# Relu and row mean over 67 MB: six tiles taken by blocks of rows in two passes, relu on ScalarE and row sums on VectorE

## The chip, the cores and the metric

The kernel runs on 1 core of one Trainium2 chip. The metric is the device time of an execution in microseconds (us). Before the change it is 164.05 us, the median of 3 runs (163.62 to 164.06). The profile is one execution recorded by the hardware; its span is about 2 us shorter than the time. All times compared below are of fast runs at a granted clock of 1.0 (the share of the full TensorE clock that the profile shows).

## The reference

```python
x = np.random.randn(32, 512, 1024).astype(np.float32)     # 67.11 MB
relu_x = np.maximum(x, 0)
out = np.mean(relu_x, axis=-1).astype(np.float32)         # 32 x 512
```

That is 16384 rows of 1024 numbers. Each of the 128 partitions takes 128 rows, in 8 tiles of 16 rows: a tile is 128 x 16 x 1024 x 4 bytes = 8.4 MB.

## The kernel before

A row is one instruction: relu and sum together, with an accumulator output. Even rows go to ScalarE, odd ones to VectorE. Tiles 0 to 6 are loaded whole, into three buffers in turn; the last tile (7) comes in pieces of 8, 4, 2 and 1 rows and three pieces of the last row, so that little work is left when the last bytes land.

```python
def act_row(nc, src, acc):
    nc.scalar.activation(out=src, in_=src, func=ACT.Relu, accum_out=acc)

def dve_row(nc, src, acc, init=None):
    nc.vector.tensor_scalar(
        out=src, in0=src, scalar1=0.0, scalar2=init,
        op0=ALU.max, op1=ALU.add, accum_out=acc,
    )
...
    in_pool = pools.enter_context(tc.tile_pool(name="in", bufs=3))
    res_pool = pools.enter_context(tc.tile_pool(name="res", bufs=1))
    sums = res_pool.tile([P, J], F32)
    res = res_pool.tile([P, J], F32)
    part = res_pool.tile([P, 10], F32)

    def rows(xt, lo, n, j0):
        for k in range(lo, lo + n):
            j = j0 + k
            (dve_row if j % 2 else act_row)(nc, xt[:, k, :], sums[:, j:j + 1])
...
    for t in range(full):                      # full = 7
        j0 = t * NB                            # NB = 16
        xt = in_pool.tile([P, NB, D], F32, name="xt")
        nc.sync.dma_start(out=xt, in_=xr[:, j0:j0 + NB, :])
        rows(xt, 0, NB, j0)
...
    # the last piece; part[:, 7:8] is ScalarE's share, already times inv
    dve_row(nc, last[:, 768:], part[:, 8:9], init=part[:, 6:7])
    nc.vector.scalar_tensor_tensor(
        out=res[:, J - 1:J], in0=part[:, 8:9], scalar=inv, in1=part[:, 7:8], op0=ALU.mult, op1=ALU.add,
    )
    nc.sync.dma_start(out=outr, in_=res)
```

Of the kernel before, what the change touches and what calls it, by code (L numbers as in the profile page):

```python
# [1 line left out]

# [4 lines left out]

F32 = mybir.dt.float32
ALU = mybir.AluOpType
ACT = mybir.ActivationFunctionType  # L10
# [15 lines that stand above are left out]
def issue_ahead_of_entry_barrier(nc):  # L26


    entry, body = nc.cur_f.blocks[0].instructions, None
    for block in nc.cur_f.blocks[1:]:  # L30
        for k, ins in enumerate(block.instructions):
            if ins.opcode == "DMACopy":
                body, load = block.instructions, k
                break
        if body is not None:
            break
    first = body[load]
    assert first.engine == mybir.EngineType.SP and not first.sync_info.on_wait
    assert all(i.opcode == "DMACopy" or i.engine != first.engine for i in body[:load])
    del body[load]  # L40
    at = next(k for k, i in enumerate(entry) if i.engine == first.engine and i.opcode == "Drain")
    entry.insert(at, first)


@with_exitstack
def kernel(
    ctx: ExitStack,
    tc: tile.TileContext,
    x: bass.AP,
    out: bass.AP,  # L50
):
    nc = tc.nc
    P = nc.NUM_PARTITIONS
    xf = x.flatten_outer_dims()
    R, D = xf.shape
    assert R % P == 0
    J = R // P
    inv = 1.0 / D
    xr = xf.rearrange("(p j) d -> p j d", p=P, j=J)
    outr = out.flatten().rearrange("(p j) -> p j", p=P, j=J)  # L60
    xlast = xr[:, J - 1, :]

    NB = 16
    full = J // NB - 1

    row_pieces = [8, 4, 2, 1]
    assert sum(row_pieces) == NB - 1
    col_pieces = [512, 256, 256]
    assert sum(col_pieces) == D

    pools = ctx.enter_context(ExitStack())
# [12 lines that stand above are left out]
    def finish(lo, hi):  # L84
        nc.gpsimd.tensor_scalar(  # L85
            out=res[:, lo:hi], in0=sums[:, lo:hi], scalar1=inv, scalar2=0.0, op0=ALU.mult, op1=ALU.add,
        )

    for t in range(full):
        j0 = t * NB  # L90
        xt = in_pool.tile([P, NB, D], F32, name="xt")
        nc.sync.dma_start(out=xt, in_=xr[:, j0:j0 + NB, :])  # L92
        rows(xt, 0, NB, j0)

    j0 = full * NB
    xt = in_pool.tile([P, NB, D], F32, name="xt")
    prev, last = xt[:, NB - 2, :], xt[:, NB - 1, :]
    lo = 0
    for n in row_pieces:
        nc.sync.dma_start(out=xt[:, lo:lo + n, :], in_=xr[:, j0 + lo:j0 + lo + n, :])  # L100
        lo += n
    c = 0
    for w in col_pieces:
        nc.sync.dma_start(out=last[:, c:c + w], in_=xlast[:, c:c + w])
        c += w

    finish(0, j0)
    lo = 0
    for n in row_pieces[:-1]:
        rows(xt, lo, n, j0)  # L110
        lo += n
    finish(j0, j0 + lo)



    act_row(nc, prev[:, :512], part[:, 0:1])
    dve_row(nc, prev[:, 512:], part[:, 1:2])
    nc.gpsimd.tensor_scalar(  # L118
        out=res[:, J - 2:J - 1], in0=part[:, 0:1], scalar1=part[:, 1:2], scalar2=inv, op0=ALU.add, op1=ALU.mult,
    )  # L120
    act_row(nc, last[:, :256], part[:, 2:3])
    dve_row(nc, last[:, 256:512], part[:, 3:4])
    nc.gpsimd.tensor_scalar(  # L123
        out=part[:, 4:5], in0=part[:, 2:3], scalar1=inv, scalar2=0.0, op0=ALU.mult, op1=ALU.add,
    )
    act_row(nc, last[:, 512:640], part[:, 5:6])
    dve_row(nc, last[:, 640:768], part[:, 6:7], init=part[:, 3:4])
    nc.scalar.activation(  # L128
        out=part[:, 7:8], in_=part[:, 5:6], func=ACT.Identity, scale=inv, bias=part[:, 4:5],
# [7 lines that stand above are left out]
    pools.close()  # L137
    tc.close()
    tc.compile()
    issue_ahead_of_entry_barrier(nc)  # L140


# [1 line left out]
_INS = ['x']  # L144
_OUTS = [((32, 512), 'float32')]


# [23 lines left out]
```

## Time and profile before

| what | before |
|---|---|
| time, median | 164.05 us |
| span of the profile | 162.1 us |
| VectorE busy | 74.7 us (46%) |
| ScalarE busy | 69.6 us (43%) |
| HBM read over the span | 414 GB/s |
| a tile's arrival | 19.3 to 19.8 us |
| both engines' work on a tile, side by side | 9.2 us |

"Busy" is an average over the whole span and says only who is not the bound. What decides is the last two rows: a tile needs twice as long to arrive as to be used up. The prediction below shows the lines for this. Two more lines belong to the instructions that the change replaces. They are groups by shape; after the bar stand the busy us and the mean ns of one, then the idle time in front.

```profile
L20 DVE TENSOR_SCALAR_CACHE_REDUCE xt<-xt 128x1024 f32<-128x1024 f32 x63 | 72.6, 1215 | 84.6 <-DMA xt<-in_x_dram 84.3
L15 ACT ACTIVATE xt<-xt 128x1024 f32<-128x1024 f32 x63 | 65.6, 1042 | 88.6 <-DMA xt<-in_x_dram 88.6
```

A row costs 1.2 us on VectorE and 1.0 us on ScalarE, and nearly all the idle time of both ends on the arrival of a load.

### The profile page before, as it was taken

To read this page: it belongs to the slowest core of one execution; us is meant where nothing else is said; L and a number is where in the kernel's file an instruction comes from. 1 tells how busy PE (TensorE), PEld (TensorE's weight loads), DVE (VectorE), ACT (ScalarE), POOL (GpSimd) and SP (SyncE) were. 2 spreads that over 40 slices of the span, in tenths; PEclk is the share of its full clock that TensorE was granted. 3 is DMA by queue.
4 is the path that set the end of the run, shared out by engine and by line. 5 is a ranking of instruction groups with operands and counts; after the bars stand their busy time and mean duration, and the time that the engine had idled before them with its cause. 6 is when DMAs were issued, how large, how long until landed. Compare 5 with 4: busy or idle time off the path is not lost.

```text
span 162.1 us, 358 instructions
## 1 busy us (share of the span) xinstructions
DVE 74.7 (46%) x135; ACT 69.6 (43%) x134; POOL 1.2 (1%) x8
## 2 busy tenths in 40 slices
DVE  0000049700795009930199102990049800698993
ACT  3000049500793009910199002980049600696882
POOL 0000000000000000000000000000000000000001
DMA  8996996997997998998998999899898897998980
GB/s 275 501 485 291 518 501 291 501 501 323 469 518 340 437 518 356 420 518 356 420 520 374 404 501 404 388 501 404 388 518 388 388 518 332 437 445 384 420 311 17
DMA packets 2162, 67.19 MB, mean 415 GB/s; under 512 B 240, under 2 KB 624, under 8 KB 880
## 3 DMA queue, kind: packets, MB, share of 16 engines
q1 hardware_dynamic: 2160, 67.18, 96.6%
q14 instruction: 2, 0.02, 0.0%
HBM read 67.11 MB, written 0.07 MB: 414 GB/s over the span
## 4 chain that ended last, share of the span: by engine, by line
DMA 84%; DVE 13%; SPq 1%; issue 0%; DVEq 0%
DMA xt<-in_x_dram 84%; DVE xt L20 13%; SPq L100 1%; DVE res L132 0%; DVEq L20 0%; DVEq L132 0%; SPq L92 0%
## 5 line engine op out<-in xcount | busy, mean ns | idle before, releaser
L20 DVE TENSOR_SCALAR_CACHE_REDUCE xt<-xt 128x1024 f32<-128x1024 f32 (+1 forms) x65 | 73.7, 1195 | 84.7 <-DMA xt<-in_x_dram 84.3
L15 ACT ACTIVATE xt<-xt 128x1024 f32<-128x1024 f32 (+1 forms) x66 | 67.0, 1015 | 88.7 <-DMA xt<-in_x_dram 88.6
L15 ACT ACTIVATION_READ_ACCUMULATOR xt<-xt 128x1 f32 x66 | 12.3, 186 | 0.0
L20 DVE DVE_READ_ACCUMULATOR xt<-xt 128x1 f32 x65 | 5.4, 83 | 0.0
L85 POOL TENSOR_SCALAR res<-sums 128x112 f32<-128x112 f32 (+1 forms) x2 | 0.5, 252 | 156.7 <-DVE xt L20 156.7
L15 ACT ACT_TABLE_LOAD x1 | 1.3, 1283 | 0.8 <-PEq L155 0.8
L20 DVE TENSOR_SCALAR_CACHE_REDUCE xt<-xt,part 128x128 f32<-128x128 f32 (+1 forms) x2 | 0.8, 412 | 0.1
L128 ACT ACTIVATE part<-part 128x1 f32<-128x1 f32 x1 | 0.3, 294 | 0.1
L118 POOL TENSOR_SCALAR res<-part 128x1 f32<-128x1 f32 x1 | 0.3, 264 | 0.5 <-ACT xt L15 0.5
L132 DVE SCALAR_TENSOR_TENSOR res<-part 128x1 f32<-128x1 f32 x1 | 0.2, 159 | 0.1
L123 POOL TENSOR_SCALAR part<-part 128x1 f32<-128x1 f32 x1 | 0.2, 191 | 0.1
L20 DVE DVE_READ_ACCUMULATOR xt<-xt,part 128x1 f32 x2 | 0.2, 83 | 0.0
L155 POOL MEMSET const-bfloat16-1.0<- 128x1 bf16 x1 | 0.1, 101 | 0.0
L155 POOL MEMSET const-uint8-127<- 128x1 uint8 x1 | 0.1, 101 | 0.0
L155 POOL MEMSET const-float32-0.0<- 128x1 f32 x1 | 0.1, 98 | 0.2 <-issue 0.2
L155 POOL MEMSET const-float32-1.0<- 128x1 f32 x1 | 0.1, 98 | 0.0
## 6 DMA issues: line engine op xcount, KB each, us to landing
xt<-in_x_dram SPq DMA_DIRECT2D x1, 4096.0 KB, 39.0
xt<-in_x_dram SPq DMA_DIRECT2D x1, 2048.0 KB, 43.5
xt<-in_x_dram SPq DMA_DIRECT2D x1, 1024.0 KB, 45.5
xt<-in_x_dram SPq DMA_DIRECT2D x1, 512.0 KB, 46.4
xt<-in_x_dram SPq DMA_DIRECT2D x1, 256.0 KB, 46.5
xt<-in_x_dram SPq DMA_DIRECT2D x2, 128.0 KB, 42.7
xt<-in_x_dram SPq DMA_DIRECT2D x7, 49.1
out_dram<-res SPq DMA_DIRECT2D x1, 64.0 KB, 1.5
```

Of the source, the lines that this page charges most:

```text
L15: nc.scalar.activation(out=src, in_=src, func=ACT.Relu, accum_out=acc)
L20: nc.vector.tensor_scalar(out=src, in0=src, scalar1=0.0, scalar2=init, op0=ALU.max, op1=ALU.add, accum_out=acc,)
L85: nc.gpsimd.tensor_scalar(out=res[:, lo:hi], in0=sums[:, lo:hi], scalar1=inv, scalar2=0.0, op0=ALU.mult, op1=ALU.add,)
L100: nc.sync.dma_start(out=xt[:, lo:lo + n, :], in_=xr[:, j0 + lo:j0 + lo + n, :])
L118: nc.gpsimd.tensor_scalar(out=res[:, J - 2:J - 1], in0=part[:, 0:1], scalar1=part[:, 1:2], scalar2=inv, op0=ALU.add, op1=ALU.mult,)
L123: nc.gpsimd.tensor_scalar(out=part[:, 4:5], in0=part[:, 2:3], scalar1=inv, scalar2=0.0, op0=ALU.mult, op1=ALU.add,)
L128: nc.scalar.activation(out=part[:, 7:8], in_=part[:, 5:6], func=ACT.Identity, scale=inv, bias=part[:, 4:5],)
L132: nc.vector.scalar_tensor_tensor(out=res[:, J - 1:J], in0=part[:, 8:9], scalar=inv, in1=part[:, 7:8], op0=ALU.mult, op1=ALU.add,)
L155: nc = _bacc.Bacc("TRN2", target_bir_lowering=False, num_devices=1)
```

## The change

The intent is to replace many small instructions by few large ones: ScalarE does relu on a block of 8 rows, then VectorE makes 8 row sums of the block in one instruction. Tile 5 is split otherwise (two blocks of 6 rows, four rows on ScalarE alone), and tile 6 and the last tile stay row by row.

```diff
+    def block(xt, lo, n, j0):
+        rs = xt[:, lo:lo + n, :]
+        nc.scalar.activation(out=rs, in_=rs, func=ACT.Relu)
+        nc.vector.tensor_reduce(
+            out=sums[:, j0 + lo:j0 + lo + n], in_=rs, axis=mybir.AxisListType.X, op=ALU.add,
+        )
...
-        rows(xt, 0, NB, j0)
+        if t < full - 2:
+            block(xt, 0, 8, j0)
+            block(xt, 8, 8, j0)
+        elif t == full - 2:
+            block(xt, 0, 6, j0)
+            block(xt, 6, 6, j0)
+            for k in range(12, NB):
+                act_row(nc, xt[:, k, :], sums[:, j0 + k:j0 + k + 1])
+        else:
+            rows(xt, 0, NB, j0)
```

## The prediction

> **What bounds the kernel now.** The work is 67.11 MB read once, with a relu and a row sum behind it. I read the page's span table first: neither compute engine is busy half the time, while the DMA row stands at 8 and 9 throughout. The bytes line gives the mean rate. (GB/s dips every third slice: with one load of 64 KB per partition, packets end in step every few microseconds, and 4 us slices beat against that. I read no stall into it.)
>
> ```profile
> span 162.1 us, 358 instructions
> DVE 74.7 (46%) x135; ACT 69.6 (43%) x134; POOL 1.2 (1%) x8
> DMA  8996996997997998998998999899898897998980
> HBM read 67.11 MB, written 0.07 MB: 414 GB/s over the span
> ```
>
> Next the busy table by stretch, cut at the moments when each 8.4 MB tile lands, which I took from the timeline (22.4, 41.7, 61.0, 80.5, 100.3, 119.7 and 139.0 us). Columns: the stretch and its length, busy us of DVE, ACT and POOL with counts, the clock, the DMA share, GB/s.
>
> ```profile
> 22.36:41.68 19.32, 9.20 (x17) 8.42 (x17) 0.00 (x0) 1.00 1.00 434
> 41.68:61.03 19.35, 9.20 (x16) 8.42 (x16) 0.00 (x0) 1.00 1.00 434
> 80.47:100.30 19.83, 9.21 (x16) 8.42 (x16) 0.00 (x0) 1.00 0.98 424
> 100.30:119.70 19.40, 9.20 (x16) 8.45 (x17) 0.00 (x0) 1.00 1.00 432
> ```
>
> A tile takes 19.3 to 19.8 us to arrive at 424 to 434 GB/s with the DMA engines 98 to 100% busy; 9.2 us of VectorE and 8.4 us of ScalarE side by side use it up. Each compute engine then waits about 10 us for the next tile. The bound is the transfer, and it has no holes to fill.
>
> The chain of waits must be read with care. It runs through 9.2 us of VectorE rows twice:
>
> ```profile
> 41.68 9.22 DVE xt L20 x16
> 50.90 0.02 SPq L92
> 50.95 49.27 DMA xt<-in_x_dram
> 100.36 9.22 DVE xt L20 x16
> 110.96 46.35 DMA xt<-in_x_dram
> ```
>
> It says that the load issued at 50.95 waited for VectorE to free its buffer. But it took 49.27 us to land where 19.35 are enough: two loads were in front of it in the queue. That release could come about 30 us later without a gap in the transfer. So the 13% of VectorE in the chain is no time to be won.
>
> Last, the end. From the timeline, VectorE at each arrival; the bracket holds the idle time ahead of a row and what ended it:
>
> ```profile
> 139.06 1.22 DVE L20 TENSOR_SCALAR_CACHE_REDUCE xt<-xt 128x1024 f32<-128x1024 f32 x1 [10.14 <-DMA xt<-in_x_dram]
> 148.78 1.22 DVE L20 TENSOR_SCALAR_CACHE_REDUCE xt<-xt 128x1024 f32<-128x1024 f32 x1 [0.52 <-DMA xt<-in_x_dram]
> 153.35 0.08 DVE L20 DVE_READ_ACCUMULATOR xt<-xt 128x1 f32 x1
> 153.56 1.22 DVE L20 TENSOR_SCALAR_CACHE_REDUCE xt<-xt 128x1024 f32<-128x1024 f32 x1
> ```
>
> From 139 us on VectorE is nearly full: 0.52 us of slack before the piece of 8 rows, 153.56 - 153.43 = 0.13 before that of 4. A delay carried past 139 us and larger than this would reach the end.
>
> **What the Trainium skill says.** (1) "VectorE: DVE Perf Modes", section "The perf-mode tier table (the rule you actually need)": a tensor_reduce runs at 1x for every data type, that is one element per cycle. The trace has no such instruction, but the row sum it replaces goes at the same pace: 685 ns for 512 elements and 1215 for 1024 is (1215 - 685)/512 = 1.035 ns an element, one cycle of the 0.96 GHz that the page gives. (2) "ScalarE: Activation LUTs", section "What ACT_TABLE_LOAD costs": an ACTIVATE with immediate operands takes 186 ns + 0.833 ns an element. The trace agrees: 186 + 1024 x 0.833 = 1039 against 1042 ns. (3) "SBUF — State Buffer", section "Who interferes with whom": DMA and compute engines use separate ports and do not contend. The stretches above fit: 434 GB/s though both engines worked for half of them. (4) "DMA: Bandwidth & Descriptors", section "Where 436 GB/s comes from": the fabric ceiling is 435 GB/s. The measured 434 sits on it, so nothing on the compute side can raise it.
>
> **The change, part by part.** Tiles 0 to 4 go from 16 row instructions to two blocks of 8 rows: ScalarE does relu on a block, then VectorE reads it once for 8 sums. Tile 5 has two blocks of 6 rows and four rows on ScalarE alone. Tile 6 and the last, piecewise tile stay. Nothing about the loads changes but when a buffer comes free.
>
> Removed: 6 tiles x 16 rows x 2 instructions (the row and its accumulator read) = 192. Added: 10 + 10 block instructions, 2 + 2 smaller ones, and 4 rows x 2 = 32. The count falls from 358 to about 198.
>
> ScalarE block: 8192 elements x 0.833 + 186 ns = 7.01 us; a 6-row one 6144 x 0.833 + 186 = 5.30. VectorE block: slope 1.04 ns and a fixed part of 1215 - 1024 x 1.04 = 150 ns give 8192 x 1.04 + 150 = 8.67 us, and 6144 x 1.04 + 150 = 6.54. These are estimates from the durations above.
>
> Work: ScalarE 69.6 - 6 x 8.42 + 10 x 7.01 + 2 x 5.30 + 4 x 1.04 = 104 us (64%). VectorE 74.7 - 6 x 9.20 + 10 x 8.67 + 2 x 6.54 = 119 us (74%). Both do more work, since relu and sum are now two passes, and stay under the span. Per tile it is 14.0 and 17.3 us against 19.4 for the arrival, so neither builds a backlog.
>
> Release of a buffer, with T the landing: first relu to T + 7.0, first sum to T + 15.7, second sum to T + 24.4 (the second relu, done at T + 14.0, is never waited for). Before, T + 9.3. So tile 3's load is issued at 22.4 + 24.4 = 46.8 instead of 31.6, and so on, 15 us later each. The load in front of it (tile 2) lands at 61.0, which leaves 14 us of queued work when the new load arrives. The last tile's pieces take tile 4's buffer, free at 100.3 + 24.4 = 124.7 instead of 109.6, while tile 6 is still streaming until 139.0. All of the added 15 us lies beside queued transfers: cost on the path zero.
>
> The handover to the end: tile 5 lands at 119.7. ScalarE: blocks to 125.0 and 130.3, four rows to 134.5. VectorE: tile 4 to 124.7, then from 125.0 to 131.6 and to 138.1. Tile 6 lands at 139.0: VectorE is free 0.9 us ahead, ScalarE 4.5 us. The tail then runs as before. The sum is zero; I expect 164.0, the median before being 164.05.
>
> **Rivals.** (a) VectorE becomes the bound. It needs a block sum above 19.4/2 = 9.7 us, 12% over my 8.67. Were the reduction at two cycles an element (17.2 us a block), tiles 0 to 4 alone would end at 29.4 + 10 x 17.2 = 201 us and the whole near 245. Against it: the page's 1x and the same slope in the row sums. For it: this case has no trace of the instruction. (b) The late release starves the queue. It would need a release beyond T + 38.7, two arrivals after the landing. Against it: 14 us of margin. If some depth of the queue itself feeds the rate, the stretches would drop from 434 to, say, 420 GB/s, and the time would be some 168. (c) A late handover. VectorE has 0.9 us in hand at 139.0 and 0.52 us more at 148.8; a block sum 8% slower (9.35 us) makes tile 4 end at 126.1 and tile 5 at 140.2, that is 1.2 us late, of which 0.7 us pass 148.8 and the end moves by about half a microsecond, 0.3%. (d) A gain: 160 instructions fewer, no accumulator reads, VectorE writing nothing back into the tile. All this is time of engines that waited 10 us a tile; the first load, the rate and the tail do not see it. To be over 2% faster the transfer would have to be 3.3 us shorter, and at 434 GB/s the 67.11 MB alone take 154.6 us, while the last landing already lies at about 157.3.
>
> **Range and chances.** The runs before spread from 163.62 to 164.06. Rival (c) and the scatter of single tiles (19.32 to 19.83 us) can add or take half a microsecond, so 163.2 to 164.9 should hold 8 times in 10. Slower by over 2% is rival (a) or (b): 4%. Faster by over 2%: 1%.
>
> **What would show it.** Right: about 198 instructions; block relus near 7.0 us and block sums near 8.7; ScalarE near 104 us and VectorE near 119 us busy; loads issued near 47, 66, 85, 105 and 125 us; stretches between landings still 19.3 to 19.8 us at 424 to 434 GB/s; the chain now through a relu and two sums and yet no longer; DMA in front of tile 6's first row. Wrong: a VectorE row at 139 us or later whose wait ended on VectorE's own tile 5 instead of the DMA, a block sum above 9.7 us, or a DMA share under 0.95 in the stretches from 61 us on, where a queue that ran dry would show.

## The result, and the profile after

The changed kernel takes 164.39 us (median of 4 runs, 164.22 to 164.44), the kernel before in the same rounds 164.01 us. The ratio is 1.0027, with a 95% interval of 1.0009 to 1.0044. Ratios here and below are the mean time of one kernel's fast runs over that of the other's of the same rounds, so not quite the ratio of the medians. By the 2% measure nothing changed, but some 0.4 us lie clear of the scatter, and the prediction had no term for them.

The head of the page of the changed kernel, with the DMA row of the 40 slices:

```profile
span 162.4 us, 201 instructions
DVE 119.0 (73%) x51; ACT 103.5 (64%) x58; POOL 1.2 (1%) x8
DMA  7997997997997999899899899799799798999970
HBM read 67.11 MB, written 0.07 MB: 414 GB/s over the span
```

Instructions fell by 157, VectorE's work rose by 44 us and ScalarE's by 34, and the bytes over the span are the same. Work of 78 us was added to the kernel without a visible price. The new instructions by shape, columns as before:

```profile
L93 DVE TENSOR_REDUCE sums<-xt 128x8 f32<-128x8192 f32 x10 | 86.4, 8681 | 37.9 <-ACT xt L92 37.9
L92 ACT ACTIVATE xt<-xt 128x8192 f32<-128x8192 f32 x10 | 69.7, 7021 | 42.1 <-DMA xt<-in_x_dram 42.1
L93 DVE TENSOR_REDUCE sums<-xt 128x6 f32<-128x6144 f32 x2 | 13.0, 6548 | 0.4 <-ACT xt L92 0.4
L92 ACT ACTIVATE xt<-xt 128x6144 f32<-128x6144 f32 x2 | 10.5, 5315 | 5.4 <-DMA xt<-in_x_dram 5.4
```

A block costs 7.02 us on ScalarE and 8.68 on VectorE. ScalarE waits for loads, VectorE for ScalarE: the two now stand one behind the other. The busy table by stretch, cut near the landings (columns as in the prediction):

```profile
61.10:80.50 19.40, 17.33 (x3) 13.95 (x2) 0.00 (x0) 1.00 1.00 432
80.50:99.84 19.34, 17.20 (x3) 13.95 (x2) 0.00 (x0) 1.00 1.00 434
99.84:119.20 19.36, 17.29 (x3) 13.95 (x2) 0.00 (x0) 1.00 1.00 433
```

VectorE works 17.2 to 17.3 us in each 19.4 us, ScalarE 14.0, and the rate is what it was. The chain of waits (start, duration, what) looks quite different all the same:

```profile
41.80 7.04 ACT xt L92
48.86 17.29 DVE sums L93 x2
66.17 33.66 DMA xt<-in_x_dram
99.91 7.04 ACT xt L92
106.97 17.29 DVE sums L93 x2
125.65 31.31 DMA xt<-in_x_dram
```

The page gives this chain as 65% DMA, 23% VectorE and 9% ScalarE; before it was 84% DMA and 13% VectorE. Taken at its word, 24.3 us twice have moved onto the critical path. They have not: the load issued at 66.17 lands 33.66 us later, although it needs 19.35, because another load stood in front of it. The longer release and the shorter stay in the queue cancel: 24.3 + 33.7 = 58.0 us now, 9.2 + 49.3 = 58.5 us before.

The timeline at the handover to the rows (start, duration, instruction, idle time in front and what ended it):

```profile
138.66 1.22 DVE L20 TENSOR_SCALAR_CACHE_REDUCE xt<-xt 128x1024 f32<-128x1024 f32 x1 [1.03 <-DMA xt<-in_x_dram]
148.36 1.22 DVE L20 TENSOR_SCALAR_CACHE_REDUCE xt<-xt 128x1024 f32<-128x1024 f32 x1 [0.49 <-DMA xt<-in_x_dram]
```

VectorE had been free for 1.03 us when tile 6 landed, and the wait ended on the DMA. In this execution tile 6 landed even 0.4 us earlier than in the profile before (138.6 against 139.0). The end shows where that went. First the kernel before:

```profile
159.23 0.08 DVE L20 DVE_READ_ACCUMULATOR xt<-xt,part 128x1 f32 x1
159.43 0.16 DVE L132 SCALAR_TENSOR_TENSOR res<-part 128x1 f32<-128x1 f32 x1
```

Then the changed kernel, the same two instructions:

```profile
158.90 0.08 DVE L20 DVE_READ_ACCUMULATOR xt<-xt,part 128x1 f32 x1
159.52 0.16 DVE L151 SCALAR_TENSOR_TENSOR res<-part 128x1 f32<-128x1 f32 x1 [0.53 <-DVE xt L20]
```

From the end of the accumulator read to the last instruction there were 0.12 us (159.43 - 159.31); now there are 0.53. ScalarE's partial sum, which the last instruction also takes, was done at 158.83, and the chain books 0.47 us of this gap as "issue": waiting for nothing that the profile shows. These 0.41 us are about the size of the whole difference, but one profile doesn't settle the account: tile 6 was 0.4 us ahead here, and the store of the results behind this instruction took 1.8 us from issue to landing instead of 1.5. It took 1.8 to 1.9 us in all four profiles that have the gap, and 1.5 in the other ten; why is not shown. The change doesn't touch the last instruction.

### The profile page after: what moved, and what is told of

Read it like the earlier page. It is cut to its first block, busy times and chain, and to the rows that moved or that the text cites. A ratio compares the mean times of both kernels' runs of the same rounds, so it can differ in the third digit from the quotient of the medians.

```text
span 162.4 us, 201 instructions
## 1 busy us (share of the span) xinstructions
DVE 119.0 (73%) x51; ACT 103.5 (64%) x58; POOL 1.2 (1%) x8
## 4 chain that ended last, share of the span: by engine, by line
DMA 65%; DVE 23%; ACT 9%; SPq 1%; issue 1%; DVEq 0%; ACTq 0%
DMA xt<-in_x_dram 65%; DVE sums L93 21%; ACT xt L92 9%; DVE xt L20 1%; SPq L119 1%; DVE res L151 0%; DVEq L151 0%; ACTq L92 0%
## 5 line engine op out<-in xcount | busy, mean ns | idle before, releaser
L93 DVE TENSOR_REDUCE sums<-xt 128x8 f32<-128x8192 f32 (+1 forms) x12 | 99.4, 8326 | 38.2 <-ACT xt L92 38.2
L92 ACT ACTIVATE xt<-xt 128x8192 f32<-128x8192 f32 (+1 forms) x12 | 80.3, 6737 | 47.5 <-DMA xt<-in_x_dram 47.5
L15 ACT ACTIVATE xt<-xt 128x1024 f32<-128x1024 f32 (+3 forms) x22 | 21.2, 962 | 7.0 <-DMA xt<-in_x_dram 6.9
L20 DVE TENSOR_SCALAR_CACHE_REDUCE xt<-xt 128x1024 f32<-128x1024 f32 (+2 forms) x17 | 18.5, 1138 | 1.9 <-DMA xt<-in_x_dram 1.7
L15 ACT ACTIVATION_READ_ACCUMULATOR xt<-xt 128x1 f32 x22 | 4.1, 187 | 0.0
L20 DVE DVE_READ_ACCUMULATOR xt<-xt 128x1 f32 x17 | 1.4, 83 | 0.0
## 6 DMA issues: line engine op xcount, KB each, us to landing
xt<-in_x_dram SPq DMA_DIRECT2D x7, 33.7
```

The source lines that it names most:

```text
L20: nc.vector.tensor_scalar(out=src, in0=src, scalar1=0.0, scalar2=init, op0=ALU.max, op1=ALU.add, accum_out=acc,)
L92: nc.scalar.activation(out=rs, in_=rs, func=ACT.Relu)
L93: nc.vector.tensor_reduce(out=sums[:, j0 + lo:j0 + lo + n], in_=rs, axis=mybir.AxisListType.X, op=ALU.add,)
```

## The experiments

Three questions: is the longer release really hidden, and by what; what is the row-by-row end worth; where do the 0.4 us come from. Each kernel gave a correct result.

### With two buffers, the changed kernel and the kernel before

If the third buffer hides the release, taking it away must cost only the changed kernel. The edit is the same in both:

```diff
-    in_pool = pools.enter_context(tc.tile_pool(name="in", bufs=3))
+    in_pool = pools.enter_context(tc.tile_pool(name="in", bufs=2))
```

> The changed kernel with two tile buffers instead of three. Theory (the third buffer is what hides the later release): a buffer is free at landing + 24.4 us, but the load in front lands at + 19.4, so the DMA runs dry for about 5 us and pays its start-up, two loads in about 45 us instead of 38.7; carried through to the last tile I get the end some 19 us later, about 183 us (178 to 188). Rival (release time doesn't matter at all, or VectorE is too fast to matter): about 164.

> The kernel before with two tile buffers instead of three. Theory: its release at landing + 9.3 us is ahead of the next landing at + 19.4, so the queue still never runs dry: 164.0, same within 0.5%. Rival (depth of the queue itself feeds the rate): slower by over 1%, with stretches between landings longer than 19.8 us.

The changed kernel took 188.12 us (ratio 1.1475, 1.1456 to 1.1494), the kernel before 163.95 (0.9999, 0.9984 to 1.0014). The rows of the changed kernel with two buffers, from the slices of its page (about 4.7 us each) and from its timeline:

```profile
DMA  9999999950998999995089999999507999999990
41.68 13.95 ACT L92 ACTIVATE xt<-xt 128x8192 f32<-128x8192 f32 x2 [5.37 <-DMA xt<-in_x_dram]
69.08 13.95 ACT L92 ACTIVATE xt<-xt 128x8192 f32<-128x8192 f32 x2 [13.45 <-DMA xt<-in_x_dram]
88.46 13.95 ACT L92 ACTIVATE xt<-xt 128x8192 f32<-128x8192 f32 x2 [5.43 <-DMA xt<-in_x_dram]
```

Now the DMA row has three holes, and the landings alternate between 27.4 us (41.68 to 69.08) and 19.4 us (69.08 to 88.46). So release time is worth nothing while a load stands in the queue, and everything when none does. My estimate of 183 us, up to 188, was too low, if only by 0.1 us at its upper end: I had a load into the empty queue at some 21 us; this kernel's chain shows 22.20 and 22.33. The kernel before with two buffers kept 431 to 435 GB/s in its stretches, so depth of queue beyond one waiting load bought nothing.

### Tiles 0 and 1 as one block of 16 rows

```diff
-            block(xt, 0, 8, j0)
-            block(xt, 8, 8, j0)
+            if t < 2:
+                block(xt, 0, NB, j0)
+            else:
+                block(xt, 0, 8, j0)
+                block(xt, 8, 8, j0)
```

> The changed kernel with tiles 0 and 1 as one block of 16 rows: relu about 13.8 us, then a sum of about 17.2 us, so their buffers come free at landing + 31 us instead of + 24.4. Theory (the release is hidden while it comes before the load in front has landed, + 38.7 us): the stretches between landings stay at 19.3 to 19.4 us. VectorE has two instructions fewer, so the fetch point falls at or behind the last instruction and the 0.5 us gap shrinks: 164.0 to 164.4. Rival (each later release costs something): slower than the changed kernel, 164.6 or more.

It took 163.67 us (ratio 0.9979, 0.9963 to 0.9995). The sum of tile 0:

```profile
36.36 17.22 DVE L93 TENSOR_REDUCE sums<-xt 128x16 f32<-128x16384 f32 x1 [36.36 <-ACT xt L92]
```

It ran to 53.58 us, so its buffer was free at landing + 31.1 us, and the stretches stayed at 19.3 to 19.4 us. A still later release costs nothing, as expected. The gap at the end shrank from 0.53 to 0.20 us, and it now ends on ScalarE (first line):

```profile
158.83 0.29 ACT L150 ACTIVATE part<-part 128x1 f32<-128x1 f32 x1 [0.42 <-ACT xt L15]
158.87 0.08 DVE L20 DVE_READ_ACCUMULATOR xt<-xt,part 128x1 f32 x1
159.15 0.16 DVE L154 SCALAR_TENSOR_TENSOR res<-part 128x1 f32<-128x1 f32 x1 [0.20 <-ACT part L150]
```

So the pause is not quite gone: ScalarE stood still for 0.42 us in front of the partial sum that the last instruction takes. All the same this is the kernel with the lowest ratio, at most 0.4% below the kernel before.

### Two passes, but row by row

This separates the split in two passes from the large instructions.

```diff
-            block(xt, 0, 8, j0)
-            block(xt, 8, 8, j0)
+            for k in range(NB):
+                block(xt, k, 1, j0)
```

> The changed kernel with the two passes of tiles 0 to 4 done row by row, relu on ScalarE and a sum on VectorE for each of 16 rows. It separates the split into two passes from the large blocks. Sums of about 1.2 us each, about 18.2 us a tile, still under 19.4; the buffer is free at about landing + 19.4 us instead of + 24.4. Theory (all this is beside the transfer; the fetch point now lies in the middle): 164.0, with no gap at the end. Rival (the blocks themselves save time on the path): slower than 164.4.

It took 163.94 us (ratio 0.9996, 0.9978 to 1.0014). The timeline of VectorE on tile 3:

```profile
81.86 18.12 DVE L93 TENSOR_REDUCE sums<-xt 128x1 f32<-128x1024 f32 x16 [1.39 <-ACT xt L92]
```

16 small sums take 18.12 us where two large ones take 17.28: the blocks save VectorE 0.84 us a tile. But row by row the first sum starts 1.2 us after the landing instead of 7.1, so the tile is finished earlier than with blocks. Neither the saving nor the earlier finish reaches the end.

### Tile 5, then tiles 5 and 6, in blocks of 8 rows

This takes away the row-by-row end step by step. For tile 5 the edit is the first pair of lines (with the second condition never true any more); for both tiles the first condition is `t < full`.

```diff
-        if t < full - 2:
+        if t < full - 1:
...
-        elif t == full - 2:
+        elif t == full:
```

> The changed kernel with tile 5 in two blocks of 8 rows as well, instead of 6 + 6 + 4 rows on ScalarE. Theory (handover): VectorE then sums tile 5 until about 143.6 us, 5 us after tile 6 has landed at 138.6; the slack of the closing rows is 0.5 + 0.2 + 0.2 us, so the end comes about 4 us later: 168.5 us (167.5 to 169.5). Rival (the end is set by the last DMA landing alone): 164.4.

> The changed kernel with tiles 5 and 6 both in two blocks of 8 rows, only the piecewise last tile by rows. Theory (handover): VectorE works through tile 6 until about 163 us, then has 7 rows and the closing pieces left, about 10.6 us; end near 175.5 us of the span, time about 177 (175 to 179). Rival (the end is set by the last DMA landing alone): 164.4.

Tile 5 in blocks took 167.73 us (ratio 1.0231, 1.0216 to 1.0246), both 177.64 us (1.0835, 1.0818 to 1.0851). VectorE with tile 5 in blocks:

```profile
126.20 17.28 DVE L93 TENSOR_REDUCE sums<-xt 128x8 f32<-128x8192 f32 x2 [2.07 <-ACT xt L92]
143.40 1.21 DVE L20 TENSOR_SCALAR_CACHE_REDUCE xt<-xt 128x1024 f32<-128x1024 f32 x1
```

and with both:

```profile
145.72 17.28 DVE L93 TENSOR_REDUCE sums<-xt 128x8 f32<-128x8192 f32 x2 [2.06 <-ACT xt L92]
162.91 1.21 DVE L20 TENSOR_SCALAR_CACHE_REDUCE xt<-xt 128x1024 f32<-128x1024 f32 x1
```

The first row behind the blocks has no bracket: it starts when VectorE is free, and no longer when its load lands. In the first case the rows of tile 6 start 4.7 us late (143.40 against 138.66) and the kernel ends 3.3 us after the changed one, after some slack of the tail. The same sums that cost nothing in the middle cost their full delay here.

### A few memsets ahead on VectorE

The 0.41 us in front of the last instruction looked like VectorE's instruction stream running over the end of a fetched piece. Short memsets in the first microseconds, where VectorE waits for tile 0, move that place without touching anything else: 16 of them took 0.49 us.

```diff
+    pad = res_pool.tile([P, 16], F32)         # 2 instead of 16 in the second run
+    for k in range(16):
+        nc.vector.memset(pad[:, k:k + 1], 0.0)
```

> The changed kernel with 16 one-column memsets put first on VectorE, which idles there for over 20 us. Theory (instruction fetch): the 0.47 us of issue time ahead of the last VectorE instruction is VectorE's instruction stream running over the end of a fetched block; 16 more instructions in front move that point back into rows of 1.2 us, where it is hidden. The gap before the last instruction falls from 0.54 us to about 0.1 to 0.2, the one instruction packet seen near 160 us moves to before 150 us, and the time falls by 0.3 to 0.4 us to about 164.0. Rival (late release or a shallower DMA queue costs the 0.4 us): nothing changes, 164.4.

> The changed kernel with only 2 such memsets. Theory (instruction fetch): the gap of about 0.5 us moves two VectorE instructions forward, still within the closing chain of short instructions, and the last instruction follows its predecessor by about 0.1 to 0.2 us; the time stays at about 164.4. Rival (the last instruction waits for something of its own, ScalarE's partial sum for example): the gap stays in front of the last instruction. Rival (late release): 164.4 too, with the gap where it was.

With 16 memsets it took 163.89 us (ratio 0.9991, 0.9975 to 1.0007), with 2 of them 163.90 us (0.9988, 0.9971 to 1.0006). The last two instructions of VectorE, with 16:

```profile
159.22 0.08 DVE L20 DVE_READ_ACCUMULATOR xt<-xt,part 128x1 f32 x1
159.41 0.16 DVE L154 SCALAR_TENSOR_TENSOR res<-part 128x1 f32<-128x1 f32 x1
```

With 2:

```profile
159.43 0.08 DVE L20 DVE_READ_ACCUMULATOR xt<-xt,part 128x1 f32 x1
159.63 0.16 DVE L154 SCALAR_TENSOR_TENSOR res<-part 128x1 f32<-128x1 f32 x1
```

Adding work made the kernel faster (the changed kernel was not in these rounds; its own ratio of 1.0009 to 1.0044 lies above both intervals), and the gap is back to 0.11 and 0.12 us. The instruction packet that I expected before 150 us with 16 memsets came at 152.4. For 2 memsets I had expected the gap to turn up two instructions earlier at the same price. It is nowhere, and the time fell: that expectation missed. A reason that would fit is that an engine's instructions are taken in while earlier ones still run, and only the last one, behind a wait, has nothing running in front of it to hide the stall. No run shows this by itself; the places counted in the next section fit it.

### The changed kernel again, and memsets in the kernel before

> The changed kernel itself, timed again beside the next three. Three kernels whose last VectorE instruction is the 51st (a row counted as two, with its accumulator read) showed a gap of 0.53 us in front of it, those where it is the 37th, 49th, 53rd or 67th did not. Theory (position in the instruction stream): the gap of 0.53 us is there again and the time is 164.2 to 164.4, some 0.3 us above the kernel before. Rival (chance of one profile): gap and difference vanish.

> The kernel before with 44 one-column memsets first on VectorE, so that its last instruction is the 135 + 44 = 179th, that is 51 + 128, and 128 instructions of 64 bytes are one packet of 8192 bytes as the trace shows it. Theory (position in the instruction stream, blocks of 128): the kernel before gets the gap of about 0.5 us in front of its last instruction, an instruction packet beside the end, and 0.3 to 0.4 us more time, 164.3. Rival (something of the blocked work, its later release or the two passes, makes the gap): no gap, 163.95.

> The kernel before with 92 memsets: the last instruction of VectorE would be 128 behind that of the changed kernel if a row with its accumulator read counted as one instruction of the stream. Theory as in the run with 44 (a row counts as two): no gap here, span about 162. If a row counts as one: the gap is here and not with 44.

> The kernel before with 172 memsets: the last instruction of VectorE is the 307th, 51 + 256. Theory (blocks of 128): the gap of about 0.5 us is here as well as with 44. If blocks are of 256 instructions: it is here and not with 44. If position is not the cause: in neither.

The changed kernel again took 164.33 us (ratio 1.003, 1.0016 to 1.0043), with the gap of 0.53 us again. So the difference is no chance of one set of runs.

The kernel before with 44 memsets took 163.97 us (1.0004, 0.9992 to 1.0017) without a gap, and with 92 and 172 there was no gap at the end either. I did not manage to bring the gap in front of this kernel's last instruction; the count that I aimed with was wrong. The run with 92 memsets shows the place. VectorE at its start:

```profile
0.85 1.75 DVE L79 MEMSET pad<- 128x1 f32 x61 [0.85 <-PEq L158]
2.99 0.92 DVE L79 MEMSET pad<- 128x1 f32 x31 [0.38 <-issue]
```

In a row of equal memsets that wait for nothing, VectorE stands still for 0.38 us after the 61st; with 172 memsets it is again after the 61st, for 0.39 us. With 44 memsets there is no such pause among them. So there is a stall at a fixed place of VectorE's stream, and I had put that place at the 51st instruction, by counting only what the profile lists.

The traces also hold each engine's semaphore waits and drains. Counted with them, and from the first instruction that the trace holds, VectorE's last instruction is number 64 of its stream in all four profiles with the gap, and the memset behind the pause is number 64 too. In the kernel before, the last instruction is number 145; 44 memsets made it 189, where 47 would have made it 192 = 64 + 128. What stood at 192 with 44 memsets, and at 320 with 172, was a drain in the closing of the program, and there the pause is: 0.45 and 0.44 us, against 0.09 in the kernel before. The drains of the two engines (shortest, median and longest ns; first and last start), in the kernel before:

```profile
L139 ACTq DRAIN  x2: 14/160/306, 158.9 to 161.6; - x2
L139 DVEq DRAIN  x2: 19/96/172, 159.5 to 161.7; - x2
```

and with 44 memsets:

```profile
L142 ACTq DRAIN  x2: 14/160/306, 158.7 to 161.4; - x2
L142 DVEq DRAIN  x2: 136/154/172, 159.3 to 161.8; - x2
```

VectorE's last drain used to start with ScalarE's and now starts 0.4 us behind it. The program ends 2.96 us after the start of its last VectorE instruction instead of 2.67, though the time of 163.97 us doesn't show it.

The rest of the record agrees. With tiles 0 and 1 as one block, the instruction in front of which ScalarE stood still is number 64 of ScalarE's stream. With 16 and with 2 memsets, number 64 of VectorE's comes right behind a row or a piece that still runs, and there is no pause. With tiles 5 and 6 in blocks, both streams are shorter than 64: no pause, and no instruction packet in the span. In the other runs such packets are of 8192 bytes (an estimate from the two figures: 64 bytes for each of 128 instructions). One of them starts 0.65 to 0.67 us after the end of each pause in the last microseconds, so the pause is not the wait for that packet. That it is the fetch of instructions in some other way is likely, not shown. (The runs with 92 and 172 were single ones of unknown state, so their times are not compared.)

## Why the prediction was right

The time was 164.39 us, predicted 164.0 with a range of 163.2 to 164.9. Point by point:

- **The bound.** Right. Up to the landing of tile 5 the stretches stayed at 19.3 to 19.4 us and 432 to 434 GB/s, with 78 us of work added beside them. The stretch of tile 6 (119.20 to 138.55 us) was as long, at 415 GB/s and a DMA share of 0.96, less than the 424 predicted; the same cut through the profile before (119.2 to 138.6) gives 414 and 0.96, so this is no effect of the change. As to the dips in GB/s that the prediction set aside: in the trace before, the packets of 64 KB took 2.42 us each and ended in groups of 16, as it said.
- **The costs.** Right to about 1%: a block relu 7.02 us (7.01 predicted), a block sum 8.68 (8.67), the 6-row ones 5.32 and 6.55 (5.30 and 6.54), ScalarE 103.5 us busy (104), VectorE 119.0 (119). The page lists 201 instructions, 3 more than my count.
- **The release hidden by the queue.** Right: the loads were issued at 46.8, 66.2, 85.5, 104.9 and 124.3 us (47, 66, 85, 105 and 125 predicted). It is shown from both sides: at landing + 31.1 us still free of charge, with two buffers 24 us dear for the changed kernel and free for the kernel before.
- **The handover.** Right: 1.03 us in hand at tile 6 (0.9 predicted). The reserve is thin, since tile 5 in blocks of 8 rows made it 2.3% slower.
- **Rivals.** VectorE as the bound fell with the 8.68 us of a sum; a starved queue with the stretches; a late handover with the wait that still ended on the DMA; a gain with the rate.
- **"The tail then runs as before. The sum is zero."** This step missed by 0.4 us. Its instructions do run as before, but the last one started 0.53 us instead of 0.12 us after the one in front of it. The memsets show that this hangs on how many VectorE instructions come ahead: with 2 more and with 16 more the gap is gone, and it is there in the other two kernels with the same number, at other times (two buffers, tile 5 in blocks). Neither the later release nor the two passes make it by themselves, since the runs without the gap have both. By the count of the streams, the change happens to leave VectorE's last instruction at number 64, where the pause stands; in the kernel before, the same pause could be brought into a closing drain. That it is the fetch of instructions is likely, but not shown. The range held these 0.4 us in part by luck: its half microsecond was meant for a late handover and for scatter.

## What to carry to other kernels

When the transfer is the bound, count for each buffer when it must be free, not when it comes free: here one load waiting in the queue hid every release up to 31 us, and a chain of waits that runs through the compute engines was no evidence against that. Keep the fine-grained work for the stretch where the queue has nothing more to hide behind, the last tile or two. And before half a microsecond at the end is blamed on a change, add or remove a few idle instructions on the engine that ends last, and see whether it stays.

## What the Trainium skill lacked or had wrong

- "Runtime: NRT & Kernel Launch", section "Instruction fetch mechanics", speaks of blocks of 16 KiB (256 instructions) and calls the crossing mostly hidden. The packets here are of 8192 bytes, and pauses of 0.37 to 0.47 us stood in front of the instructions number 64, 192 and 320 of an engine's stream, 128 apart. One of them is the gap behind the changed kernel's 0.3%. They showed in front of short instructions (the memsets, a closing drain, the last instruction behind a wait), and not behind a row that still ran.
- "DMA: Bandwidth & Descriptors", section "Where 436 GB/s comes from", says without a condition that the HBM side binds HBM loads at about 358 GB/s. With one core reading, the stretches here ran at 432 to 435 GB/s, on the page's fabric ceiling of 435. Its table for a single core (425 GB/s at 16 MB) fits better, and the note under that table has the missing condition: both cores of the HBM domain streaming.
- "VectorE: DVE Perf Modes", section "The perf-mode tier table (the rule you actually need)", lists fp32 tensor_scalar at 2x and has no row for the form with an accumulator output; only "SBUF — State Buffer", section "Who interferes with whom", leaves that form out of the two-port modes. That form took 1215 ns for 1024 elements and 685 for 512, one element a cycle, no faster than tensor_reduce at 1210 ns for 1024.
